# A hybrid recurrent layer on one core: blocks of 16 instead of 8 inverted on VectorE, a refitted list scheduler, and GpSimd's large products on ScalarE and VectorE

## The chip, the cores and the metric

One Trainium2 chip, one core of it. The metric is the device time of one launch in microseconds (us): 1104.89 us is the median of three runs of the kernel before (1103.22 to 1105.05). Below, PE is TensorE, PEld its weight loads, DVE VectorE, ACT ScalarE, POOL GpSimd and SP SyncE, whose queue issues nearly all transfers.

## The reference

One decoder layer for 256 prompt tokens and 8 sequences of 8 new tokens, 320 columns in all. One projection of the normalised input (2048 to 12416 columns) feeds two recurrences; both are projected back, gated, summed, and sent through one output projection.

```python
h = rms_norm(x, norm_g)
p = jnp.einsum('nld,dp->nlp', h, w_in)
...
# branch A, 16 heads of 64, per token
sa = jnp.einsum('nhvk,nhk->nhv', s, kk_t)
s = (s * w_t[:, :, None, :] - sa[..., None] * (kk_t * a_t)[:, :, None, :]
     + v_t[..., None] * k_t[:, :, None, :])
y_t = jnp.einsum('nhvk,nhk->nhv', s, r_t)
...
merged = (sigmoid(p[..., OFF_GA:OFF_GB]) * jnp.einsum('nlw,wd->nld', y_a, proj_a)
          + sigmoid(p[..., OFF_GB:]) * jnp.einsum('nlw,wd->nld', y_b, proj_b))
y = x + jnp.einsum('nld,de->nle', merged, w_out)
```

Branch A is computed in chunks of 64 tokens. Inside a chunk the delta rule is a unit lower triangular system of 64 by 64, so the kernel needs the inverse of such a matrix for each head and chunk. The sequences of 8 new tokens give diagonal blocks of 8 by 8.

## The kernel before, in words

**The stream.** Weights come in tiles of 1024 by 128 by DMA (`raw`, three buffers). ACT rounds each to a high part `whi`, DVE subtracts to get the low part `wlo`, and each of the 16 blocks of 128 rows takes three products of 128 by 320 into PSUM (`mps`, two buffers): high by high, high by low, low by high. These are the products `mps<-...`. A half tile has 24, a column tile 48.

**The recorded part.** After a first tile, 71 column tiles are not issued directly. `tile_of` (L1465 stands for every recorded instruction, because they are issued from one line at the end) records their loads, casts and products, and between them the work of eight steps p = 0 to 7, each with two heads of branch A (`rwkv`) and one of branch B (`hgrn`). `Recorder.add` gives each recorded operation a duration in ns (`o.cost`) and a time until its result can be used (`o.lat`). `link` finds what depends on what. `order` is a list scheduler: it plays the five engines against each other with these durations and so writes down one order per engine. On the chip each engine then runs its list in order and waits at semaphores. A product of the stream goes where nothing small is ready, so how many `mps` products stand between two small ones is the planner's estimate of how long the other engines need. `MARGIN` is an extra time that the planner adds before a small product on PE may stand.

**The inverse.** In `rwkv`, `g2` holds the 64 by 64 matrices. ACT copies their triangles to `nd`; POOL masks out the diagonal blocks of 8 by 8 (`lows`), DVE folds them into `dn` (768 rows of 8), and two transfers through DRAM (`scratch[0]`) lay each block out on one partition (`nb`, 96 blocks). DVE inverts the blocks there with elementwise products and sums (`y8`, doubling 2 to 4 to 8). Two more transfers through `scratch[1]` bring the inverses back (`ye`), POOL spreads them into `yd` and `ys`, ACT copies `yd` into `yz`. From there PE doubles the block size: `for sz in (8, 16, 32)` makes two transposes of `yd`, two products `M` by `yz` (`a<-yz,uE` in the trace) and two products `a<-pp,uB`, with a mask on DVE and a subtraction on DVE between.

**Around it.** After the inverse the first transposes, chunk recurrences (`chunks`: `rhs`, `uv`, `st`) and the sample part (`samples`) follow, then the norm of branch A (`jr_cent`, `jr_mean`) and `ya`. Four recorded tiles after the last step fill sigmoid gates, three more go to DRAM (`late`). The second stage (`L362` to `L364`) is not recorded: it streams the remaining gate columns and, from `split(ya)` on, the products `ppa` and `ppb` with `proj_a` and `proj_b`. The third stage (`po`) multiplies by `w_out`.

**GpSimd's products.** POOL also computes `bm` (128x512) in `samples`, `vm` (96x512, twice) in `hgrn`, `lows` and `yd` (128x256), each a broadcast product of two SBUF operands.

Of the kernel before, what the change touches and what calls it, by code (L numbers as in the profile page):

```python
# [69 lines left out]
class Recorder:  # L70
    APART, MARGIN, WAIT, OVER = 10, 250, 6000, 130
    LAT = {"PE": 215, "V": 45, "S": 45, "G": 80, "Y": 0}
# [13 lines left out]
    def add(self, eng, name, fn, args, kw):  # L86
        o = Op()
        o.eng, o.fn, o.args, o.kw, o.n = eng, fn, args, kw, len(self.ops)
        aps = [x for x in (*args, *kw.values()) if hasattr(x, "start_partition")]
        out = aps[0]  # L90
        free = 1
# [51 lines left out]
        elif eng == "S":  # L143
# [3 lines left out]
            if any(tuple(x.shape[1:]) == (1,) and free > 1 for x in aps[1:]):  # L147
                o.cost += 60
        elif eng == "G":
            o.cost = 950 if "dma" in name else 95 + free * 0.88 if name == "memset" else 200 + free * 1.66  # L150
            if "dma" in name:
                o.lat = 4500
        else:
            o.cost, o.lat = 380, 2600 if any(u[0].startswith("scr") for u in o.uses) else 5500
        self.ops.append(o)
        return o

    def link(self):

        writers, readers, preds = {}, {}, {}  # L160
        for o in self.ops:
            o.succ, pred = [], {}
            preds[o.n] = pred
            for name, p0, p1, m, wr, psum in o.uses:
# [47 lines left out]
    def order(self):  # L212
# [17 lines left out]
        def choose(e):  # L230
# [29 lines left out]
            can = [o for o in q if (at_[o] if e in port else o.ready) <= t_ + 30]  # L260
# [6 lines left out]
            return t_, max(can, key=worth)  # L267
# [30 lines left out]
def hybrid_step(ctx, tc, x_prompt, x_sample, state_rwkv, state_hgrn, state_shift, norm_g, w_in,  # L298
# [80 lines left out]
    with tc.tile_pool(name="start", bufs=1) as st, \  # L379
# [63 lines left out]
        id8 = ctile([128, 64], "id8")  # L443
        G.memset(id8, 0.0)
        G.memset(id8[:, 0:64:9], 1.0)
# [5 lines left out]
        lvs = st.tile([128, 3, 32], F32, name="lvs")  # L451
        lvz = ctile([128, 3, 2, 32], "lvz")
# [4 lines left out]
        for n, sz in enumerate((8, 16, 32)):  # L457
# [11 lines left out]
        G.tensor_copy(seqm[HS[1]], seqm[low_])  # L469

# [314 lines left out]
    def rwkv(p, r, k, vp, za):  # L785
# [132 lines left out]
        for h in range(2):  # L918
            for c_ in range(2):
# [3 lines left out]
        lows = at("lows", (128, 4, 8, 8), tag="pp")  # L923
        each = lambda n: seqm[:, None, :, None].to_broadcast([128, n, 8, 8])
        G.tensor_mul(lows, nd.rearrange("p a h (b j) -> p (a h) b j", j=8), each(4))
        dn = at("dn", (128, 6, 8))
        V.tensor_reduce(dn[:, 0:4], lows.rearrange("p c b j -> p c j b"), axis=mybir.AxisListType.X, op=ALU.add)
        V.tensor_reduce(dn[0:64, 4:6], g2[0:64, 4, 0].rearrange("p h (b j) -> p h j b", j=8),
                        axis=mybir.AxisListType.X, op=ALU.add)
        there = lambda t_: t_.rearrange("(c p) j -> p c j", c=6)  # L930
        whole = lambda t_: t_.rearrange("(q i) j -> q (i j)", i=8)
        Y.dma_start(there(scratch[0]), dn)
        nb = at("nb", (96, 64), tag="pp")
        Y.dma_start(nb, whole(scratch[0]))
        y8 = at("y8", (96, 64))
        V.tensor_sub(y8, id8[:96], nb)

        t8 = nb
        four = lambda o_, *d: bass.AP(y8.tensor, y8.offset + o_, [y8.ap[0], *d])
        t4 = t8[:, 0:4].rearrange("p (a i) -> p a i", i=2)  # L940
        V.tensor_mul(t4, four(2, [36, 2], [8, 2]), four(19, [36, 2], [0, 2]))
        V.tensor_add(four(3, [36, 2], [8, 2]), four(3, [36, 2], [8, 2]), t4)
        V.tensor_mul(t4, four(10, [36, 2], [1, 2]), four(1, [36, 2], [0, 2]))
        V.tensor_add(four(2, [36, 2], [1, 2]), four(2, [36, 2], [1, 2]), t4)
        t64 = t8.rearrange("p (i j k) -> p i j k", j=4, k=4)
        p16 = at("p16", (96, 4, 4))
        V.tensor_mul(t64, four(4, [8, 4], [0, 4], [1, 4]), four(36, [0, 4], [1, 4], [8, 4]))
        V.tensor_reduce(p16, t64, axis=mybir.AxisListType.X, op=ALU.add)
        V.tensor_mul(t64, four(0, [8, 4], [0, 4], [1, 4]),
                     p16.rearrange("p k j -> p j k")[:, None].to_broadcast([96, 4, 4, 4]))  # L950
        V.tensor_reduce(four(4, [8, 4], [1, 4]), t64, axis=mybir.AxisListType.X, op=ALU.add)
        Y.dma_start(whole(scratch[1]), y8)
        ye = at("ye", (128, 6, 8))
# [730 lines left out]
```

## Time and profile before

| what | value |
|---|---|
| median of three runs | 1104.89 us |
| profiled execution | 1104.54 us, of which the span is 1102.8 us |
| PE busy | 1081.3 us, 98% |
| DVE busy | 750.6 us, 68% |
| ACT busy | 680.1 us, 62% |
| POOL busy | 154.6 us, 14% |
| DMA | 161.62 MB, mean 147 GB/s |

The busy time of PE is made of overlapping products: one `mps` product lasts 0.31 us in the trace, and the next starts 0.147 us after it. So the cost of an extra product is read from the starts, not from its length. A wait shows as idle time ahead of an instruction, with what released it. The span divides into a start (to 27 us), the recorded part (to about 690 us, the first stage's tail reaching into the second), the second stage, and the third (from about 975 us).

### The profile page before, as it was taken

Reading aid. Unit: us, or ns where it says so; the run is one execution under the profiler, and the core shown is the slowest. Engines: PE = TensorE matmul, PEld = TensorE weight load, DVE = VectorE, ACT = ScalarE, POOL = GpSimd, SP = SyncE. Lnnn points to the kernel's source line nnn. Section 1 sums busy time; section 2 is a strip of 40 time slices with the busy share of each in tenths; the row PEclk is TensorE's granted clock in tenths of the full one; section 3 lists DMA queues with packets and bytes.
Section 4 is the critical chain, followed back from the end, with each engine's and each line's share of the span. In section 5 each row is a group of like instructions: output and inputs, shape, how many; then the busy total and the mean of one; then the engine's idle time right before and its main releaser. Section 6 shows DMA issues by size and latency. Waiting matters only on the chain.

```text
span 1102.8 us, 23134 instructions
## 1 busy us (share of the span) xinstructions
PE 1081.3 (98%) x9020; PEld 1043.5 (95%) x9020; DVE 750.6 (68%) x1639; ACT 680.1 (62%) x1530; POOL 154.6 (14%) x328
## 2 busy tenths in 40 slices
PE   7999999999999999999999999999999999999996
PEld 6999999999998999999999999999999999998886
DVE  8878787888787788788887976644444444437532
ACT  8767776766865867857857867544444444435412
POOL 6421222311211211211311210000000000000000
PEclk9999999999999999999999999999999999999999
DMA  6743644654553554555445454555555555586502
GB/s 200 205 127 100 180 129 123 161 145 114 162 136 101 156 144 117 153 138 140 117 138 144 123 144 130 149 152 160 152 146 146 149 154 153 153 282 223 200 21 96
DMA packets 298386, 161.62 MB, mean 147 GB/s; under 512 B 37341, under 2 KB 288480, under 8 KB 297700
## 3 DMA queue, kind: packets, MB, share of 16 engines
q1 hardware_dynamic: 297908, 158.83, 50.1%
q8 instruction: 71, 1.16, 0.4%
q10 hardware_dynamic: 368, 1.31, 0.3%
q14 instruction: 39, 0.32, 0.1%
HBM read 149.41 MB, written 10.70 MB: 145 GB/s over the span
## 4 chain that ended last, share of the span: by engine, by line
PE 95%; ACT 2%; DMA 1%; DVE 1%; issue 0%; POOL 0%; DVEq 0%; SPq 0%; ACTq 0%
PE mps L1465 45%; PE a L1465 9%; PE mps L362 5%; PE mps L364 5%; PE mps L363 5%; PE b L1465 3%; PE po L1555 3%; PE po L1556 3%; PE po L1557 3%; PE ppa L363 2%; PE ppa L364 2%; PE ppa L362 2%; PE ppb L362 2%; PE ppb L363 2%; PE ppb L364 2%; PE y L1465 1%
## 5 line engine op out<-in xcount | busy, mean ns | idle before, releaser
L1465 PE MATMUL mps<-hhi,wlo 128*128 128x320 f32 x1136 | 358.9, 316 | 0.0
L1465 PE MATMUL mps<-hhi,whi 128*128 128x320 f32 x1136 | 357.0, 314 | 0.5 <-ACT pad L1465 0.5
L1465 PE MATMUL mps<-hlo,whi 128*128 128x320 f32 x1136 | 357.3, 314 | 0.0
L1465 PEld LDWEIGHTS mps<-hhi,wlo 128*128 128x128 f32 x1136 | 213.7, 188 | 2.3 <-issue 1.5
L1465 PEld LDWEIGHTS mps<-hhi,whi 128*128 128x128 f32 x1136 | 213.8, 188 | 2.0 <-issue 0.8
L1465 PEld LDWEIGHTS mps<-hlo,whi 128*128 128x128 f32 x1136 | 213.7, 188 | 1.5 <-issue 0.8
L1465 DVE TENSOR_TENSOR wlo<-raw,whi 128x1024 fp32r<-128x1024 f32 x140 | 173.6, 1240 | 21.0 <-ACT whi L1465 19.7
L1465 ACT CAST whi<-raw 128x1024 fp32r<-128x1024 f32 x140 | 146.4, 1045 | 63.2 <-PE mps L1465 56.7
L352 ACT CAST whi<-raw 128x1024 fp32r<-128x1024 f32 x82 | 86.0, 1049 | 147.8 <-PE mps L363 94.3
L353 DVE TENSOR_TENSOR wlo<-raw,whi 128x1024 fp32r<-128x1024 f32 x82 | 100.5, 1225 | 110.1 <-ACT whi L352 110.1
L362 PE MATMUL mps<-hhi,whi 128*128 128x320 f32 x400 | 123.9, 310 | 1.0 <-ACT whi L352 1.0
L364 PE MATMUL mps<-hhi,wlo 128*128 128x320 f32 x400 | 123.7, 309 | 0.2 <-DVE wlo L353 0.2
L363 PE MATMUL mps<-hlo,whi 128*128 128x320 f32 x400 | 123.8, 309 | 0.0
L362 PEld LDWEIGHTS mps<-hhi,whi 128*128 128x128 f32 x400 | 75.1, 188 | 1.3 <-ACT whi L352 1.3
L364 PEld LDWEIGHTS mps<-hhi,wlo 128*128 128x128 f32 x400 | 75.1, 188 | 0.4 <-DVE wlo L353 0.4
L363 PEld LDWEIGHTS mps<-hlo,whi 128*128 128x128 f32 x400 | 75.2, 188 | 0.0
L1544 DVE TENSOR_TENSOR wlo<-raw,whi 128x1024 fp32r<-128x1024 f32 x32 | 38.4, 1222 | 36.0 <-ACT whi L1543 35.8
L1543 ACT CAST whi<-raw 128x1024 fp32r<-128x1024 f32 x32 | 33.1, 1052 | 47.7 <-PE po L1560 21.1
L1555 PE MATMUL po<-whi,mhi 128*128 128x512 f32 x128 | 50.0, 391 | 0.0
L1556 PE MATMUL po<-whi,mlo 128*128 128x512 f32 x128 | 50.0, 391 | 0.0
L1557 PE MATMUL po<-wlo,mhi 128*128 128x512 f32 x128 | 50.0, 391 | 0.0
L362 PE MATMUL ppa<-yah,whi 128*128 128x320 f32 x128 | 40.1, 314 | 0.1
(444 smaller groups left out, 2100.2 us busy)
## 6 DMA issues: line engine op xcount, KB each, us to landing
raw<-in_w_in_dram SPq DMA_DIRECT2D x194, 512.0 KB
raw<-in_w_out_dram SPq DMA_DIRECT2D x32, 512.0 KB
raw<-in_proj_a_dram SPq DMA_DIRECT2D x16, 512.0 KB
raw<-in_proj_b_dram SPq DMA_DIRECT2D x16, 512.0 KB
s<-in_state_hgrn_dram SPq DMA_DIRECT2D x8, 512.0 KB
out_dram<-s SPq DMA_DIRECT2D x8, 512.0 KB
s<-in_state_rwkv_dram SPq DMA_DIRECT2D x8, 256.0 KB
out_dram<-s SPq DMA_DIRECT2D x8, 256.0 KB
```

Of the source, the lines that this page charges most:

```text
L352: S.copy(hi[:, ks], raw[:, ks])
L353: sub.tensor_sub(lo[:, ks], raw[:, ks], hi[:, ks].bitcast(F32))
L362: T.matmul(dst, hi[:, q, :], xhi[:, k, :], start=(k == 0), stop=False)
L363: T.matmul(dst, hi[:, q, :], xlo[:, k, :], start=False, stop=False)
L364: T.matmul(dst, lo[:, q, :], xhi[:, k, :], start=False, stop=(k == nk - 1))
L1465: o.fn(*o.args, **o.kw)
L1543: S.copy(hi, raw)
L1544: V.tensor_sub(lo, raw, hi.bitcast(F32))
L1555: T.matmul(pt, h, hi, start=first, stop=False)
L1556: T.matmul(pt, l, hi, start=False, stop=False)
L1557: T.matmul(pt, h, lo, start=False, stop=end)
```

## The change

**Blocks of 16.** `dn` gets 16 columns, 48 partitions hold a block of 16 by 16 each, and DVE inverts them in the layout `y16`: a scaling to the negative, ones on the diagonal by a POOL memset, the step to 2 by 2 as before, and for n = 4 and n = 8 a product, a sum, a product, a sum on n by n by n elements (twice for n = 4). The loop on PE is `for sz in (16, 32)`.

**Engines.** `lows`, `yd` and `ys` go from POOL to DVE. `bm` and `vm` become four ACT operations each with a per-partition scale. Seven copies and scalings of 64x64 per step (two of `rhs`, five of `uv`) go from DVE to ACT, and five small copies (`fh`, `fq`) from DVE to POOL.

**The planner.** Its durations are refitted: for an output on all 128 partitions a part of the duration (`DRAIN`) moves from the engine's time to the time until the result can be used; sums over the free axis cost by the number of inputs; two accesses of different engines to one PSUM bank are ordered. `MARGIN` goes from 250 to 400. `order` may leave an engine idle up to `AHEAD` = 300 ns for an operation of higher rank, filling the gap with one that is short enough.

```diff
-    APART, MARGIN, WAIT, OVER = 10, 250, 6000, 130
-    LAT = {"PE": 215, "V": 45, "S": 45, "G": 80, "Y": 0}
+    APART, MARGIN, WAIT, OVER = 10, 400, 6000, 45
+    AHEAD, SLIP = 300, 0
+    LAT = {"PE": 215, "V": 40, "S": 40, "G": 65, "Y": 0}
+    DRAIN = {"V": 85, "S": 100, "G": 65}
...
+        if eng in self.DRAIN and not o.dma:
+            if name == "tensor_reduce":
+                n = 1
+                for d in aps[1].shape[1:]:
+                    n *= d
+                o.cost += (n - free) / 0.96
+            if out.shape[0] == 128:
+                o.cost -= self.DRAIN[eng]
+                o.lat += self.DRAIN[eng]
+            else:
+                o.cost += 13
...
-                        if hit(u):
+                        if hit(u) or psum and u[3].eng != o.eng:
...
-                q.succ.append((o, data))
+                q.succ.append((o, data or q.eng in self.DRAIN and q.eng != o.eng))
...
-            can = [o for o in q if (at_[o] if e in port else o.ready) <= t_ + 30]
+            best = max((o for o in q if at_[o] <= t_ + self.AHEAD), key=worth)
+            if at_[best] > t_ + 30:
+                short = [o for o in q if at_[o] <= t_ + 30 and at_[o] + o.cost <= at_[best] + self.SLIP]
+                if short:
+                    best = max(short, key=worth)
+            return t_, best
...
-        lows = at("lows", (128, 4, 8, 8), tag="pp")
+        lows = at("lows", (128, 4, 4, 16), tag="pp")
-        G.tensor_mul(lows, nd.rearrange("p a h (b j) -> p (a h) b j", j=8), each(4))
+        V.tensor_mul(lows, nd.rearrange("p a h (b j) -> p (a h) b j", j=16), each(4))
...
-        V.tensor_sub(y8, id8[:96], nb)
+        V.tensor_scalar(y16, nb, -1.0, 0.0, op0=ALU.mult, op1=ALU.add)
+        G.memset(y16[:, 0:256:17], 1.0)
...
+        for n in (4, 8):
+            t_ = at("t3", (48, n, n, n), tag="big")
+            pw_ = at("p64", (48, n, n), tag="uQ")
+            for o_ in range(0, 16, 2 * n):
+                at_ = lambda i, j: 17 * o_ + 16 * i + j
+                V.tensor_mul(t_, four(at_(0, n), [16, n], [0, n], [1, n]), four(at_(n, n), [0, n], [1, n], [16, n]))
+                V.tensor_reduce(pw_, t_, axis=mybir.AxisListType.X, op=ALU.add)
+                V.tensor_mul(t_, four(at_(0, 0), [16, n], [0, n], [1, n]),
+                             pw_.rearrange("p k j -> p j k")[:, None].to_broadcast([48, n, n, n]))
+                V.tensor_reduce(four(at_(0, n), [16, n], [1, n]), t_, axis=mybir.AxisListType.X, op=ALU.add)
...
-        for sz in (8, 16, 32):
+        for sz in (16, 32):
...
-            G.tensor_mul(bm, bk[:, 4, None].to_broadcast([128, 4, 128]), seq4[:, :, None].to_broadcast([128, 4, 128]))
+            for si in range(4):
+                S.activation(bm[:, si], bk[:, 4], AF.Copy, scale=seq4[:, si:si + 1])
...
-            G.tensor_mul(vm[0:96], v3[:, g, None].bitcast(F32).to_broadcast([96, 4, 128]),
-                         seq4[0:96, :, None].to_broadcast([96, 4, 128]))
+            for si in range(4):
+                S.activation(vm[0:96, si], v3[:, g].bitcast(F32), AF.Copy, scale=seq4[0:96, si:si + 1])
```

The order of before on DVE, in the third step (p = 2), where the blocks of 8 are inverted: `y` is `y8`, `pp` and `p` are its scratch, `R`, `F`, `w` and `o` belong to the other branch.

```order
L1465 TENSOR_TENSOR pp_515<-y_0_517 96x4
L1465 TENSOR_TENSOR F_529<-F_529 128x8x16
L1465 TENSOR_TENSOR y_0_517<-y_0_517,pp_515 96x2x2
L1465 TENSOR_TENSOR w_0_531<-w_0_531,q_483 128x16x8
L1465 TENSOR_TENSOR pp_515<-y_0_517 96x64
L1465 TENSOR_TENSOR w_0_531<-w_0_531,f_485 128x16x8
L1465 TENSOR_TENSOR wlo<-raw,whi 128x1024
L1465 TENSOR_REDUCE p_0_518<-pp_515 96x16
L1465 TENSOR_TENSOR R_530<-R_530,F_529 128x4x32
L1465 TENSOR_TENSOR pp_515<-y_0_517,p_0_518 96x64
L1465 TENSOR_TENSOR F_529<-F_529 128x4x32
L1465 TENSOR_REDUCE y_0_517<-pp_515 96x4x4
```

The same place on DVE in the changed kernel: `uK` is now `y16`, `big` holds the n by n by n products, `uQ` their sums.

```order
L1489 TENSOR_TENSOR big_511<-uK_490 48x64
L1489 TENSOR_REDUCE uQ_472<-big_511 48x16
L1489 TENSOR_TENSOR wlo<-raw,whi 128x1024
L1489 TENSOR_TENSOR big_511<-uK_490,uQ_472 48x64
L1489 TENSOR_REDUCE uK_490<-big_511 48x4x4
...
L1489 TENSOR_TENSOR big_511<-uK_490 48x512
L1489 TENSOR_REDUCE uQ_472<-big_511 48x64
L1489 TENSOR_TENSOR wlo<-raw,whi 128x1024
L1489 TENSOR_TENSOR big_511<-uK_490,uQ_472 48x512
L1489 TENSOR_REDUCE uK_490<-big_511 48x8x8
```

Before, an operation of the other branch or of the weights stands behind nearly every operation of the inversion. Now its 17 operations stand together, with two `wlo` between them and nothing else, and the two pairs on 512 elements are new.

The order of before on PE at the end of the recorded part: the last small product of the last step (`jr_mean`) stands among products of the second stage, and the first product that needs all of `ya` (`ppa`) comes 23 rows later.

```order
L362 MATMUL mps<-hhi,whi 128x320
L1465 MATMUL a_497<-rl_495,jr_mean 128x320
L363 MATMUL mps<-hlo,whi 128x320
...
L363 MATMUL mps<-hlo,whi 128x320
L362 MATMUL ppa<-yah,whi 128x320
L364 MATMUL mps<-hhi,wlo 128x320
```

The same place in the changed kernel:

```order
L1489 MATMUL mps<-hhi,wlo 128x320
L1489 MATMUL a_494<-rl_492,jr_mean 128x320
L1489 MATMUL mps<-hhi,whi 128x320
...
L383 MATMUL mps<-hlo,whi 128x320
L382 MATMUL ppa<-yah,whi 128x320
L383 MATMUL ppa<-yal,whi 128x320
```

The last small product now stands among recorded products (L1489, the new number of L1465), and 145 rows lie between it and the first `ppa` instead of 23. In the middle of the program the distance on PE from a step's `a<-arp,bk` products to its first transposes of `yd` is nearly what it was: on average 161 `mps` products before and 167 now (third step: 165 and 174).

More of the change, by code (lines that the diff above doesn't have):

```diff
@@ L259, in choose @@
                 return max(t_, o.ready), o
-            can = [o for o in q if (at_[o] if e in port else o.ready) <= t_ + 30]
+            if e not in port:
+                at_ = {o: max(now, o.ready) for o in q}
             def worth(o):
@@ L940, in rwkv @@
[L940 to L947, printed above, removed]
@@ L1362, in hybrid_step @@
     scr = ctx.enter_context(tc.tile_pool(name="scr", bufs=1, space=bass.MemoryType.DRAM))
-    scratch = [scr.tile([768, 8], F32, name=f"scr{j}", tag=f"scr{j}") for j in range(2)]
+    scratch = [scr.tile([768, 16], F32, name=f"scr{j}", tag=f"scr{j}") for j in range(2)]
     late = [scr.tile([128, NT], F32, name=f"scrg{m}", tag=f"scrg{m}") for m in range(NLATE)]
```

64 lines of the change are left out of this document (32 added, 32 removed).

## The prediction, made before the changed kernel had run

> **What bounds the kernel now.** I read the page first: the span, the busy times and the chain that ended last.
>
> ```profile
> span 1102.8 us, 23134 instructions
> PE 1081.3 (98%) x9020; PEld 1043.5 (95%) x9020; DVE 750.6 (68%) x1639; ACT 680.1 (62%) x1530; POOL 154.6 (14%) x328
> PE 95%; ACT 2%; DMA 1%; DVE 1%; issue 0%; POOL 0%; DVEq 0%; SPq 0%; ACTq 0%
> ```
>
> PE is the bound: the chain that set the end is PE work for 95%. So only two kinds of time can change: products that PE no longer makes, and waits in which PE stands still. Next I read the windows by stage. The columns are the stretch, its length, and the busy time of PE, PEld, DVE, ACT and POOL with their instructions, then the granted clock, the DMA share and GB/s.
>
> ```profile
> 27.00:660.00 633.00, 628.00 (x6120) 614.81 (x6119) 513.59 (x1291) 460.29 (x1160) 135.70 (x280) 1.00 0.50 139
> 660.00:694.00 34.00, 32.31 (x311) 30.02 (x309) 23.24 (x57) 25.72 (x69) 1.66 (x2) 1.00 0.49 139
> 694.00:699.00 5.00, 4.78 (x21) 4.55 (x22) 4.21 (x7) 4.55 (x9) 0.00 (x0) 0.66 0.55 164
> 699.00:1060.00 361.00, 361.00 (x2264) 346.78 (x2263) 173.11 (x206) 158.29 (x227) 0.00 (x0) 1.00 0.54 165
> ```
>
> From 699 us on PE has no gap and the change touches nothing there. In the recorded part PE lacks 5.0 us of 633, and at its seam with the second stage 1.7 us of 34 and a stretch of 5 us at a clock of 0.66. Third, the waits of PE between 27 and 700 us: what waited, for whom, us in total, times, longest.
>
> ```profile
> PE b L1465 <- issue: 1.9, 1, 1.9
> PE a L1465 <- DVE yz L1465: 1.2, 2, 0.6
> PE a L1465 <- POOL yd L1465: 1.0, 1, 1.0
> PE mps L362 <- ACT whi L352: 1.0, 1, 1.0
> PE a L1465 <- ACT uv L1465: 0.5, 1, 0.5
> PE mps L1465 <- ACT pad L1465: 0.5, 1, 0.5
> PE a L1465 <- issue: 0.4, 1, 0.4
> PE mps L364 <- DVE wlo L353: 0.2, 1, 0.2
> ```
>
> Six gaps (issue, yz twice, yd, pad, issue) lie before 660 us: 1.9 + 1.2 + 1.0 + 0.5 + 0.4 = 5.0 us. Three (whi, uv, wlo) lie in the seam: 1.7 us. A gap costs more than its idle time, because the overlap of the products is lost too:
>
> ```profile
> 691.92 0.31 PE L364 MATMUL mps<-hhi,wlo 128*128 128x320 f32 x1
> 693.22 0.41 PE L362 MATMUL mps<-hhi,whi 128*128 128x320 f32 x1 [0.99 <-ACT whi L352]
> ```
>
> Start to start this is 1.30 us where undisturbed products are 0.147 apart (below), so 1.15 lost with 0.99 idle: 0.16 us more per gap.
>
> **Part 1: one doubling less on PE.** The step for size 8 goes: per step p two transposes of `yd`, two products `a<-yz,uE` and two `a<-pp,uB` (each product of 128x128 in full float32 is two records). The timeline of PE shows what they cost inside the stream: start, duration, line, tile.
>
> ```profile
> 167.48 0.31 PE L1465 MATMUL mps<-hhi,whi 128*128 128x320 f32 x1
> 167.63 0.38 PE L1465 MATMUL a<-ident,yd 128*128 128x128 f32 x2
> ...
> 167.99 0.31 PE L1465 MATMUL mps<-hhi,wlo 128*128 128x320 f32 x1
> ...
> 168.29 0.31 PE L1465 MATMUL mps<-hlo,whi 128*128 128x320 f32 x1
> 168.44 0.61 PE L1465 MATMUL a<-yz,uE 128*128 128x128 f32 x4
> 168.80 0.39 PE L1465 MATMUL mps<-hhi,wlo 128*128 128x320 f32 x1
> 169.03 0.31 PE L1465 MATMUL mps<-hhi,whi 128*128 128x320 f32 x1
> ...
> 169.76 0.31 PE L1465 MATMUL mps<-hhi,wlo 128*128 128x320 f32 x1
> 169.90 0.61 PE L1465 MATMUL a<-pp,uB 128*128 128x128 f32 x4
> ...
> 170.50 0.30 PE L1465 MATMUL mps<-hlo,whi 128*128 128x320 f32 x1
> ```
>
> From 169.03 to 169.76 lie five products of the stream, 0.146 each. The transposes stretch two such steps (0.29) to 167.99 - 167.48 = 0.51: 0.22 us. The two pairs stretch two steps to 169.03 - 168.29 = 0.74 and 170.50 - 169.76 = 0.74: 0.45 us each, the slow first product after them (0.23 instead of 0.147) included. So a level costs 0.22 + 0.45 + 0.45 = 1.12 us, and over eight steps **-8.9 us**. Nothing hides this: PE has no other gap to put it in. At most it is 0.6 us less, where such products stand beside other small ones and share the switch of 0.08 us.
>
> **Part 2: the seam.** In the order of before 23 PE rows lie between the last small product of step 7 and the first `ppa`, now 145. So the tail of step 7 is done some 122 x 0.147 = 18 us earlier against the stream, and the splitting of `ya`, behind which ACT and DVE make the second stage's weights, lies beside stream products. The three gaps cost 1.7 + 3 x 0.16 = 2.2 us. In 694 to 699 us there are 21 products where 34 would fit; 13 x 0.147 = 1.9, less 0.4 for the gap at `wlo` already counted: 1.5 us. I let both go: **-3.7 us**. Late next is nothing that the profile shows before 1060 us. The clock is the weaker half: it read 1.00 in the other three stretches, so also around the gap of 1.9 us, and fell here, where three gaps lie close together. [...]
>
> **Part 3: the longer chain on DVE.** Instead of PE, DVE doubles from 8 to 16. That costs no PE time unless the first transposes of a step wait. In the third step, the one with the gap at `yd`, the chain of before was this (one row from each place):
>
> ```profile
> 233.14 0.22 DVE L1465 TENSOR_TENSOR y<-id,pp 96x64 f32<-96x64 f32 x1
> 239.12 0.21 DVE L1465 TENSOR_REDUCE y<-pp 96x16 f32<-96x64 f32 x1
> 239.35 0.33 SPq L1465 DMA_DIRECT2D scr<-y  x1
> 242.36 0.37 SPq L1465 DMA_DIRECT2D ye<-scr  x1
> 247.22 1.25 POOL L1465 TENSOR_TENSOR yd<-ye,seqm 128x256 f32<-128x256 f32 x1 [2.35 <-DMA ye<-scr]
> ```
>
> DVE took 239.33 - 233.14 = 6.2 us, nine short operations with others between; the transfers 3.0 and 4.9 us; POOL 1.25. Prices for the new DVE work come from groups of before (count, then busy us and mean ns):
>
> ```profile
> L1465 DVE TENSOR_TENSOR y<-id,pp 96x64 f32<-96x64 f32 x8 | 1.7, 218 | 0.2
> L1465 DVE TENSOR_TENSOR pp<-y 96x64 f32<-96x64 f32 x8 | 2.2, 274 | 0.0
> L1465 DVE TENSOR_REDUCE p<-pp 96x16 f32<-96x64 f32 x8 | 1.7, 209 | 0.0
> L1465 DVE TENSOR_REDUCE dn<-pp 128x32 f32<-128x256 f32 x8 | 5.3, 659 | 4.0 <-POOL pp L1465 4.0
> L1465 DVE TENSOR_TENSOR wlo<-raw,whi 128x1024 fp32r<-128x1024 f32 x140 | 173.6, 1240 | 21.0 <-ACT whi L1465 19.7
> L1465 ACT CAST whi<-raw 128x1024 fp32r<-128x1024 f32 x140 | 146.4, 1045 | 63.2 <-PE mps L1465 56.7
> ```
>
> Read in order, an element costs (1240 - 218) / 960 = 1.06 ns, so 512 elements take 0.70 us. That is the low bound. The products of the inversion read one operand in steps of a row: 274 instead of 218 for 64 elements, 0.88 ns per element more, so 512 take 0.70 + 0.45 = 1.15 us. The sum `dn<-pp`, also read in steps, has 659 for 256 elements where 218 + 192 x 1.06 = 422 would do: 0.93 ns more, the same price. I take 1.15 for the two products and 0.70 for the two sums, which read in order. [...]
>
> The chain is then: the scaling of 256 elements 0.42, four operations on 8 elements 0.6 (an estimate under the 0.21 of 64 elements), four pairs on 64 elements 4 x (0.27 + 0.21) = 1.9, the two pairs on 512 2 x 1.15 + 2 x 0.70 = 3.7, and the two `wlo` that the order puts between, 2 x 1.15 = 2.3: 8.9 us instead of 6.2. Against that, `lows` and `yd` as DVE operations of 128x256, some 0.42 us each by the same price, in place of POOL's (1.25 here): about 1.0 us saved in all. The transfers carry twice the bytes in the same number of pieces or fewer, 64 bytes instead of 32 at the small end; nothing in the trace prices this, between 0 and 1 us more. I take 0. So the chain grows by 1.7 us, and the order gives it 167 instead of 161 products on average, 6 x 0.147 = 0.9 us more. That leaves 0.8 us less room per step. One step in eight waited before; in the others there was room, how much I leave open. If all eight lacked the 0.8, that would be 6.4 us; if only the third did, 0.8. I take **+1.5 us** for it. The other five gaps before 660 us I leave as they are: they lie in chains that the change only reorders, with 150 ns more margin but durations that are closer and so leave less unplanned room.
>
> **Part 4: other moved work.** `bm` and `vm` go to ACT: twelve operations on 128 columns per step, each between nothing and half a cast (0.5 us), so at most 6 us of a step's 633 / 8 = 79. ACT was busy 460 of 633 us, with 22 us free per step, and its wait of 56.7 us in the row above is for PE to release `whi`, so casts are ahead of the stream and this costs 0. If that cover went, each late cast would cost what the gap at `whi` cost, 1.15 us. What queues behind: `bm` shares its buffer with the n by n by n products, so ACT now waits there for the end of DVE's chain, with a cast behind it. POOL, busy 136 of 633 us, gives four large products away for five small copies and a memset of the diagonal, which costs nothing on PE. SP has as many transfers as before.
>
> **The sum.** -8.9 - 3.7 + 1.5 = -11.1 us on the profiled execution of 1104.54 (its span of 1102.8 and 1.7 around it), which lies 0.35 us under the median of the runs, so I make no correction: **1093.4 us**.
>
> **The rivals.** *All gaps close.* The planner's new durations fit, and its margin of 400 catches the rest. For it, the timeline of DVE:
>
> ```profile
> 229.96 1.22 DVE L1465 TENSOR_TENSOR wlo<-raw,whi 128x1024 fp32r<-128x1024 f32 x1
> 231.10 1.33 DVE L1465 TENSOR_TENSOR R<-F 128x320 f32<-128x320 f32 x1
> ```
>
> `wlo` holds DVE for 1.14 us and ends at 1.22; the old plan held DVE for 1024 / 0.96 + 157 = 1224 ns, the new one for 85 less. Against it: the gap at `issue` of 1.9 us has no releaser that a plan could move, and strided reads are not in the new durations either. 1104.5 - 8.9 - 3.7 - (5.0 + 6 x 0.16 = 6.0) = 1085.9 us. Chance 0.2.
>
> *Products go, gaps move.* ACT, loaded with up to 6 us more per step and waiting at `bm`, makes casts or `pad` copies late about once a step, at the price of the gap at `pad`, 0.5 + 0.16 = 0.66: 8 x 0.66 = 5.3 us on top, 1098.7 us. Chance 0.18. For it: ACT stood behind three of the nine gaps. Against it: its 56.7 us of room.
>
> *Slower: every step's first transposes wait.* PE takes its list in order, so when `yd` is late the whole stream stands. With a wait w in each step the time is 1104.5 - 12.6 - 1.2 + 8w. It is no gain from w = 1.7 us, and slower by more than 0.2% from w = 2.0. Reaching that takes the 0.8 of part 3 without the room of the seven other steps, transfers 1 us slower, and 0.5 from waiting for POOL's memset in the chain; at their sum, w = 2.3, it is 1109.1 us. Against it: that room was there in seven of eight steps, and the order sets the margin anew. Chance 0.12, half of it within 0.2%.
>
> **How the numbers follow.** The forecast, 1090 to 1097, has 0.5. The range takes in the first rival at 1085.9 with 1.4 us of doubt in parts 1 and 3 and the second at 1098.7 with the clock's 1.5 us: 1084.5 to 1100.5, leaving out most of the third. 0.2%, 2.2 us, is about what a measurement of this kernel can tell from no change. Faster by more than that: 0.5 + 0.2 + 0.18 = 0.88; within it 0.06; slower 0.06.
>
> **What would show it.** In the new profile: 32 records fewer each of `a<-yz,uE` and `a<-pp,uB`; no PE gap between the last recorded product and `ppa`, and a clock of 1.00 there; DVE products on 512 elements at 1.1 to 1.2 us; waits of PE on DVE `yd` of 1 to 5 us in all. It is wrong if waits on `yd` or `whi` exceed 9 us, or if the recorded part is not shorter by about the level's 8.9 us plus the difference in gaps.

## The result, and the profile after

The changed kernel takes 1097.48 us (median of 5 runs, 1095.81 to 1100.13), the kernel before in the same comparison 1105.05 us (5 runs, 1103.22 to 1106.62): a ratio of 0.9929, 95% interval 0.9908 to 0.995. The forecast was 1093.4 us, 4.1 less. The profiled execution took 1097.48 us too, so it stands for the median.

The page of the changed kernel, then its windows by stage (columns as before):

```profile
span 1095.8 us, 23048 instructions
PE 1072.2 (98%) x8940; PEld 1035.4 (94%) x8940; DVE 764.8 (70%) x1607; ACT 723.5 (66%) x1658; POOL 113.3 (10%) x325
PE 83%; DVE 8%; ACT 4%; issue 2%; DMA 2%; DVEq 0%; SPq 0%; ACTq 0%
```

```profile
27.00:660.00 633.00, 624.47 (x6079) 610.27 (x6078) 538.55 (x1300) 513.87 (x1329) 96.23 (x282) 1.00 0.51 140
660.00:687.00 27.00, 27.00 (x271) 26.74 (x270) 11.74 (x14) 13.94 (x25) 0.00 (x0) 1.00 0.55 160
687.00:694.00 7.00, 5.78 (x38) 5.52 (x38) 6.08 (x8) 6.97 (x12) 0.00 (x0) 1.00 0.44 133
694.00:1060.00 366.00, 366.00 (x2281) 350.51 (x2280) 175.69 (x211) 158.93 (x230) 0.00 (x0) 1.00 0.54 164
```

PE has 80 records fewer, and is still the bound. But between 27 and 660 us it now lacks 8.5 us where it lacked 5.0, and 1.2 us are still missing at the seam. Which waits those are, from the view of PE's waits between 27 and 700 us:

```profile
PE b L1489 <- issue: 4.6, 3, 2.1
PE a L1489 <- DVE yd L1489: 2.8, 5, 0.7
PE mps L1489 <- issue: 1.0, 1, 1.0
PE ppa L382 <- ACT yah L1511: 0.8, 1, 0.8
PE ppa L383 <- DVE yal L1512: 0.4, 1, 0.4
```

The waits on `yz`, `uv`, `pad`, `whi` and `wlo` are gone. The waits on `yd` went from one to five. And "issue", time in which PE waits for nothing that the profile shows, went from 2.3 us to 5.6. The timeline of PE has these four places (idle time in brackets):

```profile
173.38 0.26 PE L1489 MATMUL b<-ks,s 128*32 128x64 f32 x3 [1.30 <-issue]
252.81 0.22 PE L1489 MATMUL b<-ket 128*32 128x32 f32 x2 [1.14 <-issue]
330.80 0.24 PE L1489 MATMUL b<-ks,s 128*32 128x64 f32 x1 [2.12 <-issue]
409.98 0.30 PE L1489 MATMUL mps<-hhi,wlo 128*128 128x320 f32 x1 [1.01 <-issue]
```

All four stand at or behind the end of the same piece of work, the burst of some 140 small records that one call of `side_by_side` issues in each step; the four other steps have no such wait. Behind the longest of them, the window of 3.5 us shows a granted clock of 0.51:

```profile
332.00:335.50 3.50, 3.50 (x16) 3.50 (x15) 2.29 (x9) 2.69 (x11) 0.21 (x1) 0.51 0.02 5
```

The 16 products in it would be 24 at 0.147 us; the drop costs some 1.7 us (3.4 us at half speed). Before, such a drop stood at the seam; there the clock is now 1.00.

The seam, from ACT's timeline: the last gate tile `f` is made, and the first cast of the split waits.

```profile
681.30 0.97 ACT L1489 ACTIVATE f<-f 128x320 f32<-128x320 f32 x2
687.03 2.61 ACT L1511 CAST yah<-ya 128x640 fp32r<-128x640 f32 x4 [2.58 <-DMA scrg<-f]
```

What `yah` waits for is not step 7's chain, but the transfer that writes `f` to DRAM: `yah` takes SBUF that `f` gives up.

### The profile page after: what moved, and what is told of

Read it like the earlier page. It is cut to its first block, busy times and chain, and to the rows that moved or that the text cites. A ratio compares the mean times of both kernels' runs of the same rounds, so it can differ in the third digit from the quotient of the medians.

```text
span 1095.8 us, 23048 instructions
## 1 busy us (share of the span) xinstructions
PE 1072.2 (98%) x8940; PEld 1035.4 (94%) x8940; DVE 764.8 (70%) x1607; ACT 723.5 (66%) x1658; POOL 113.3 (10%) x325
## 3 DMA queue, kind: packets, MB, share of 16 engines
q8 instruction: 70, 1.15, 0.4%
## 4 chain that ended last, share of the span: by engine, by line
PE 83%; DVE 8%; ACT 4%; issue 2%; DMA 2%; DVEq 0%; SPq 0%; ACTq 0%
PE mps L1489 34%; PE a L1489 8%; PE mps L382 5%; PE mps L384 5%; PE mps L383 5%; PE b L1489 3%; PE po L1579 3%; PE po L1580 3%; PE po L1581 3%; DVE wlo L1489 3%; PE ppa L383 2%; PE ppb L382 2%; PE ppb L383 2%; PE ppb L384 2%; PE ppa L384 2%
## 5 line engine op out<-in xcount | busy, mean ns | idle before, releaser
L1489 PE MATMUL mps<-hhi,wlo 128*128 128x320 f32 x1136 | 358.2, 315 | 1.0 <-issue 1.0
L1489 PE MATMUL mps<-hhi,whi 128*128 128x320 f32 x1136 | 357.8, 315 | 0.0
L1489 PE MATMUL mps<-hlo,whi 128*128 128x320 f32 x1136 | 357.1, 314 | 0.0
L1489 PEld LDWEIGHTS mps<-hhi,whi 128*128 128x128 f32 x1136 | 214.1, 188 | 2.3 <-issue 1.5
L1489 PEld LDWEIGHTS mps<-hlo,whi 128*128 128x128 f32 x1136 | 214.2, 189 | 2.1 <-issue 1.5
L1489 PEld LDWEIGHTS mps<-hhi,wlo 128*128 128x128 f32 x1136 | 214.2, 189 | 1.9 <-issue 1.2
L1489 DVE TENSOR_TENSOR wlo<-raw,whi 128x1024 fp32r<-128x1024 f32 x140 | 170.7, 1220 | 24.4 <-ACT whi L1489 22.7
L1489 ACT CAST whi<-raw 128x1024 fp32r<-128x1024 f32 x140 | 145.7, 1042 | 26.6 <-PE mps L1489 24.0
```

The lines of the kernel that those rows point to most:

```text
L1489: o.fn(*o.args, **o.kw)
```

## The experiments

Two theories for the missing 4.1 us. *Instruction stream:* the waits at "issue" depend on where in PE's instruction stream a burst begins. The page's row of the queue that carries instructions (packets, MB, share) says in what pieces they come:

```profile
q8 instruction: 70, 1.15, 0.4%
```

1.15 MB in 70 packets is 16.4 KB each; PE has 8,940 weight loads, as many products and some 80 waits in its stream, 17,960 in all. If these bytes are PE's alone, one takes 64 and a piece holds 256: an estimate from the row and the counts. Against it: *place in the program*: the bursts coincide with transfers, ACT's load or an order that the planner made worse. They are told apart by products of 32x32 that are put on PE at the start: they move every later instruction in the stream and, beyond a later start, change nothing else. "Position" means the count of PE's instructions at the burst's first product, modulo 256.

**84 tiny products ahead of the changed kernel.**

```diff
             V.memset(ones.bitcast(F32), 1.0)
+            for _ in range(84):
+                T.matmul(wps[:32, :32], ones[:32, :32], ones[:32, :32], start=True, stop=True)
```

> The changed kernel with 84 tiny products (32x32, one record each) put on PE at the start, where PE has nothing to do. In the changed kernel PE stands 5.6 us in all at 173, 253, 331 and 410 us, each time at the end of the burst of some 140 small records of a step and each time with no releaser. Theory (instruction stream): PE's instructions come in pieces of 256, and a burst that crosses from one piece to the next at the wrong place uses a piece up before the next is there. Counted from the first instruction of PE, modulo 256, the eight bursts start at 142, 190, 199, 180, 151, 109, 115, 74 now; the four that stand are those between 145 and 205. 84 records more are 168 instructions more: 54, 102, 111, 92, 63, 21, 27, 242. By this theory all four waits go, 5.6 + 4 x 0.16 = 6.2 us, and with them the drop of the granted clock behind the longest, about 1.8 us: 1089.5 us (1088.5 to 1091.5). Rival (place in the program: transfers, load of ACT, the planner's order): the order is the same, so the four waits stay and the time is that of the changed kernel, 1097.5, or up to 5 us more if the 84 products delay the start.

1094.73 us (ratio to before 0.9897, 0.9881 to 0.9913). Its waits of PE between 27 and 720 us, whole:

```profile
PE a L1491 <- DVE yd L1491: 4.5, 7, 1.4
PE ppa L382 <- ACT yah L1513: 0.6, 1, 0.6
PE ppa L383 <- DVE yal L1514: 0.4, 1, 0.4
```

No wait at "issue" is left, and the clock stays at 1.00: the theory holds, the rival doesn't. The time missed the 1089.5 because the tiny products did delay the start, and the waits on `yd` grew by 1.7 us. The start is read from one early product that all kernels have, first in the changed kernel, then in this one:

```profile
24.59 0.27 PE L683 MATMUL cps<-ident,rows 128*128 128x128 f32 x1
```

```profile
28.04 0.27 PE L685 MATMUL cps<-ident,rows 128*128 128x128 f32 x1
```

From there to the first `ppa` the changed kernel takes 663.2 us, this one 657.0. The sum closes: 1097.5 - 6.2 (waits with lost overlap) - 1.7 (clock) + 3.4 (start) + 1.7 + 2 x 0.16 (`yd`) = 1095.0, 0.3 off the measured time.

**22 of them.** The same edit with 22, which fit into the time in which PE waits for its first operands and cost 0.15 us of start.

> The changed kernel with 22 tiny products on PE at the start: the bursts start at 186, 234, 243, 224, 195, 153, 159, 118 modulo 256. Theory (instruction stream): the waits move, to the steps 0, 4, 5 and 6 (186, 195, 153, 159), and steps 1, 2, 3 and 7 have none; about the changed kernel's time, 1095 to 1099 us. Rival (place in the program): the waits stay in the steps 1, 2, 3 and 4 at about 173, 253, 331 and 410 us.

One run, 1092.7 us, below the 1095 to 1099 expected. Waits at "issue": 1.45 us at 92.9 (step 0) and 1.42 us at 557.4 (step 6); none in the other steps. So the waits did move, but to two of the four steps named. The position alone is too coarse a rule. The trace has a finer one. Each window of the DMA view in which the instruction queue moved a packet brackets its start to 0.1 us; for the wait at 173.38 in the changed kernel these are the rows of 170.8 to 170.9 and of 174.5 to 174.6 us:

```profile
q8 instruction: 1, 0.02, 61.6%
q8 instruction: 1, 0.02, 73.3%
```

One piece starts at 170.9, PE runs dry at 172.1 and goes on at 173.4, and the next piece starts at 174.6. Read so for all kernels here, the 14 waits at "issue" that stand at a burst end 2.3 to 2.7 us after such a packet starts, and no two packets start closer than 3.2 us. A burst of 280 instructions runs in some 2 us where nothing holds it (2.06 us from 481.25 us in the changed kernel). In 13 of the 14 the next piece starts 3.4 to 4.2 us after that packet, in one (669 us in the next kernel) 8.2 us. Pairs at 3.6 us without a wait exist too, so a close pair alone does not make a wait, and what makes a piece come late is not shown. Three waits at "issue" of 0.4 to 0.6 us, ahead of products `a<-pp,uB`, stand 12 us or more behind a packet and are of another kind; the 0.4 us of the kernel before is one of them.

**98 of them ahead of the kernel before.**

> The kernel before with 98 tiny products on PE at the start and nothing else. Its bursts start at 250, 78, 96, 186, 250, 210, 224, 255 now, with one wait of 1.9 us in step 3 (186); with 196 instructions more at 190, 18, 36, 126, 190, 150, 164, 195. Theory (instruction stream): waits of 1 to 2 us in the steps 0, 4, 5, 6 and 7 and none in step 3, so 4 waits more of about 1.5 + 0.16 us each: some 6.6 us slower than the kernel before, 1111 us (1108 to 1114). Rival (place in the program): the wait of 1.9 us stays in step 3 and the time is 1105.

1114.94 us, 1.008 of the kernel before (1.0063 to 1.0096), just above the 1108 to 1114 expected. The wait in step 3 is gone; the steps 0, 4, 5, 6 and 7 have waits of 0.58, 1.94, 0.23, 0.71 and 1.78 us. Of the 10.4 us between the profiled executions 4.2 are the later start (28.85 against 24.63), 3.3 the waits at "issue" (2.3 before, 5.6 now) and 1.1 the waits on `yd`, before the lost overlap. An edit that adds no work behind the start thus made the same program slower, in part through these waits. Beside it, the lesson for part 2: the clock dropped for 3.4 us after the 1.78 and not after the 1.94, so the length of a gap alone does not decide it. The drops in the kernel before (0.50 from 695.16 to 698.57 us), in the changed one and in this one are 3.41 us long each; what sets that length is not shown.

**The seam: the gates that go to DRAM first.**

```diff
-        for m in range(NFILL):
-            tile_of(OFF_GA + 128 * m, lambda ps, m=m: sigm(sga[:, m, :], ps))
         for m, (pool, key) in enumerate(((at, "za"), (bt, "q"), (bt, "f"))[:NLATE]):
...
             tile_of(OFF_GA + 128 * (NFILL + m), post)
+        for m in range(NFILL):
+            tile_of(OFF_GA + 128 * m, lambda ps, m=m: sigm(sga[:, m, :], ps))
```

> The changed kernel with the last seven tiles of the recorded part in another order: the three whose gates go to DRAM first, the four that stay in SBUF last; and 45 tiny products at the start, which by the first theory keep all bursts (142, 187, 172, 165, 191, 136, 142, 187 without them) clear: 232, 21, 6, 255, 25, 226, 232, 21. Theory for the seam: its two waits (0.8 and 0.4 us) come from the transfer of the last gate tile to DRAM, whose SBUF the first cast of the split takes; with that transfer early they go, 1.7 us with the lost overlap: 1089.5 - 1.7 = 1087.8 us, and no wait at the first ppa. Rival for the seam: step 7's chain or ACT's load sets it, and the waits stay at about 1.2 us: 1089.5.

1090.45 us (0.9859, 0.984 to 0.9878). All waits of PE between 27 and 720 us:

```profile
PE a L1491 <- DVE yd L1491: 3.9, 6, 1.3
```

The seam is clean and no wait at "issue" is left, so the transfer of `f` was the cause at the seam. Against the expected 1087.8 stand a start that is 1.4 us later and the waits on `yd`.

**The waits on `yd`: a price for strided reads.**

```diff
+            far = [x for x in aps[1:] if "PSUM" not in str(x.space) and [s for s, c in x.ap[1:] if c > 1][-1:] > [3]]
+            if far:
...
+                o.cost += n * 0.88
```

> The changed kernel; its planner now adds 0.88 ns per element to a DVE operation that reads SBUF in inner steps of more than three elements (the price that the trace shows). 8 of the 20 products that warm PE up at the start are replaced by 33 tiny ones, which takes about as long and puts the bursts at 230, 6, 6, 21, 222, 250, 227, 253 modulo 256, clear of the instruction waits. Beside it stands the changed kernel with 84 tiny products, which has no instruction waits either: 1094.7, of which some 3.4 us are its later start, so 1091.3. Theory: the waits on yd, 4.5 us there, come from a chain on DVE that takes longer than its planner thinks; with the price they fall below 1 us: 1087.5 us (1086 to 1089). Rival: they come from the transfers before yd or from PE's own arrival, which the price does not touch: they stay at 2.5 to 4.5 us, 1091.

1087.38 us (0.9842, 0.9827 to 0.9857), as expected, and no wait on `yd`:

```profile
PE ppa L388 <- ACT yah L1519: 1.1, 1, 1.1
PE ppa L389 <- DVE yal L1520: 0.4, 1, 0.4
```

Behind these two gaps the clock drops again: it reads 0.50 from 678.3 to 681.6 us.

**A control: the same time, spread over all DVE operations.**

```diff
+            o.cost += 10
```

> A control for the price: the changed kernel, whose planner adds 10 ns to every DVE operation (some 190 of them per step, 1.9 us, about what the price for reads in steps adds to one step's chain of DVE, but not there), and 34 tiny products at the start, which put the bursts at 244, 255, 8, 254, 216, 239, 235, 239 modulo 256. Theory (the waits on yd come from the price that is missing in the chain before yd): the waits on yd stay at 2 to 5 us, 1091 us (1090 to 1093). Rival (any new order, or any slack on DVE, removes them): below 1 us, 1088.

1089.29 us (0.9847, 0.9828 to 0.9866); waits on `yd` 1.8 us in four steps. Neither side is met: less than the 2 to 5 expected, more than the rival's 1.

**All three together.** Price, order of the gates, and 22 tiny products.

> The three causes taken together: the price of 0.88 ns per element for DVE's reads in steps, the three gates that go to DRAM ahead of the four that stay in SBUF, and 22 tiny products at the start, which put the bursts at 224, 0, 0, 15, 216, 2, 13, 34 modulo 256, clear of the instruction waits. The kernel with the price alone took 1087.4 us; it had waits of 1.1 and 0.4 us at the seam, 1.8 with the lost overlap, and a stretch of 3.4 us at half the clock just behind them, 1.7 us. Theory: both go, and 0.4 us of its later start: 1083.5 us (1082.5 to 1085). Rival for the clock: it drops on its own account somewhere: 1085.2. Rival for the seam: the other order brings waits of its own, 1087.

1088.06 us (0.9832, 0.9815 to 0.985): no gain over the price alone. The seam is clean, the clock stays at 1.00, there is no wait at "issue". But `yd` is back, in two steps:

```profile
PE a L1497 <- DVE yd L1497: 3.5, 2, 2.1
```

The planner is the one with the price, and PE's order is the same into step 4 (to 400 us) but for one swap; the other order of the gates reached back into the last steps. DVE's timeline shows that here it is the transfer that is late:

```profile
552.02 0.43 DVE L1497 TENSOR_TENSOR yd<-ye,own 128x256 f32<-128x256 f32 x1 [2.29 <-DMA ye<-scr]
631.05 0.42 DVE L1497 TENSOR_TENSOR yd<-ye,own 128x256 f32<-128x256 f32 x1 [2.17 <-DMA ye<-scr]
```

So the price is not shown to be what removed the waits; with it they stayed out in one order and not in the other.

**The planner waits longer for the small transfers.**

```diff
-            o.cost, o.lat = 380, 2600 if any(u[0].startswith("scr") for u in o.uses) else 5500
+            o.cost, o.lat = 380, 4600 if any(u[0].startswith("scr") for u in o.uses) else 5500
```

> The kernel with the three causes taken together, which took 1088.1 us, with one number of the planner changed: the small transfers through DRAM land after 380 + 4600 ns, not 380 + 2600. 22 tiny products ahead and 38 in place of 7 that warm PE up put the bursts at 130, 244, 119, 83, 44, 5, 220, 87 modulo 256, clear of the instruction waits. In the kernel with the three causes PE waited 3.5 us for yd in steps 6 and 7, and there DVE waited 2.3 and 2.2 us for the transfer of ye, which came 3.9 and 4.6 us after its issue where the planner has 3.0. Theory (the rest of the waits on yd is the landing of the two transfers): the waits on yd go, 3.5 + 0.3 us: 1084.2 us (1083 to 1085.5). Rival (yd's waits are a matter of where the plan happens to put the chain, whatever it takes the transfers for): waits on yd of 2 us or more somewhere, 1087 or more.

1138.82 us, 1.0303 of the kernel before (1.0288 to 1.0317). The waits on `yd` are gone, and something worse has come. PE's waits, the first two rows:

```profile
PE mps L1499 <- ACT pad L1499: 24.3, 4, 6.5
PE mps L1499 <- ACT i L1499: 6.7, 4, 1.9
```

One of the four, followed from PE to ACT to DVE:

```profile
339.54 0.64 PE L1499 MATMUL mps<-hhi,whi 128*128 128x320 f32 x1 [5.98 <-ACT pad L1499]
```

```profile
333.45 1.04 ACT L1499 CAST whi<-raw 128x1024 fp32r<-128x1024 f32 x1 [2.47 <-PE mps L1499]
337.53 1.28 ACT L1499 ACTIVATE big<-bk,seq 128x128 f32<-128x128 f32 x4 [3.03 <-DVE uK L1499]
339.00 0.49 ACT L1499 COPY pad<-mps 128x256 f32<-128x256 f32 x2 [0.19 <-DVE r L1499]
```

```profile
335.71 1.07 DVE L1499 TENSOR_TENSOR big<-uK,uQ 48x512 f32<-48x512 f32 x1
336.81 0.68 DVE L1499 TENSOR_REDUCE uK<-big 48x64 f32<-48x512 f32 x1
337.52 0.33 DVE L1499 TENSOR_TENSOR fq<-f,fh 32x8 fp32r<-32x8 f32 x2
337.87 0.50 DVE L1499 TENSOR_TENSOR dif<-pad 128x328 f32<-128x328 f32 x1
338.41 0.69 DVE L1499 SCALAR_TENSOR_TENSOR r<-dif,cols,pad 128x256 f32<-128x256 f32 x2
```

PE's bank of PSUM is full until ACT copies it into `pad`. ACT takes its list in order, and ahead of that copy stands `bm` (`big<-bk,seq`), whose buffer DVE's chain still reads: `bm` starts when the last sum ends. But `bm` is done at 338.81, and the copy still waits, for DVE's `r`. There is one `pad`; `dif` and `r` read what it held before, and they stand behind the whole chain in DVE's list. So without `bm` the copy would have started no earlier: what holds PE for 6 us is the chain on DVE ahead of the readers of `pad`. It is so in all four waits. Behind the wait the clock is at half besides (0.50 from 339.54 to 343.20 us, some 1.8 us lost). Neither theory had that.

**The planner alone, on the kernel before** (the class `Recorder` of the changed kernel in the program before, and 93 tiny products in place of 20 that warm PE up).

> The kernel before with the planner of the changed kernel alone (blocks of 8 and POOL's products stay), and the 20 products that warm PE up replaced by 93 tiny ones, which puts the bursts at 30, 56, 38, 43, 2, 7, 222, 212 modulo 256, clear of the instruction waits. Theory (the planner closes its gaps, the level's work is a separate 8.9 us): the waits at yz, yd, pad, uv and whi (4.1 us idle, 5.1 us with the lost overlap) go, the instruction waits of 2.3 us too, the clock's drop at the seam (1.5 us) too; some 1.2 us at the seam and 1 us on yd come in: 1105 - 5.1 - 2.6 - 1.5 + 2.2 = 1098 us (1096 to 1100). Rival (the new durations move gaps only): only the instruction waits go: 1102.5.

1099.41 us (0.9948, 0.993 to 0.9965): the theory, within its range. PE's waits in it are 2.4 us in five places, and it starts 2.1 us later than the kernel before (26.68 against 24.63).

**The large products `bm` and `vm` back on POOL** (as before; the same 93 tiny products).

> The changed kernel with the products bm and vm back on POOL, as before, and 93 tiny products for the 20 that warm PE up, which puts the bursts at 42, 38, 52, 8, 16, 245, 17, 214 modulo 256, clear of the instruction waits. Theory (the twelve ACT operations per step lie beside PE's work): on PE nothing changes by it, 1091.3 us as the changed kernel without instruction waits (1090 to 1093). Rival (POOL's large products hold DVE's port and delay its chain): waits on yd grow to 8 us or more, 1095 or more. Second rival (ACT's load costs the changed kernel time): faster than 1089.5.

1097.25 us (4 runs, 1094.71 to 1099.16; 0.9929, 0.9907 to 0.9951), its profiled execution 1094.71. Its waits on `yd` are 3.9 us in three steps, 5.7 us in seven places in all. So neither rival's sign: POOL's products do not push `yd` to 8 us, and the kernel is not faster than 1089.5. `port` is the planner's name for DVE's operations and POOL's holding each other up. The kernel before has such a place: `R<-F` on 128x320 takes 1.33 us at 231.10, beside `bm` on POOL (230.31 to 232.09 us), where the median of its eight is 0.48. But the time misses the theory's 1090 to 1093 too. Of the 1094.7 of the profiled execution 2.1 are a later start; what makes the other runs up to 4.5 us longer is not shown, and it hides any small effect of ACT's load. Beside the kernel before with the new planner this one has the blocks of 16 and the other moves between DVE, ACT and POOL, with the same tiny products, the same start (26.70 against 26.68 us), the same 3468 `mps` products ahead of the first `ppa` and the same engine for `bm` and `vm`: to the first `ppa` it takes 658.1 us against 663.0, 5.0 less, with 5.7 + 7 x 0.16 = 6.8 us of waits against 2.4 + 5 x 0.16 = 3.2. Without the waits the blocks and the moves are worth 5.0 + 3.6 = 8.6 us; of the two, the level alone takes work from PE.

**The change with the planner of before.**

> The changed kernel with the planner of the kernel before; 20 tiny products at the start put the bursts at 238, 85, 223, 252, 0, 5, 174, 34 modulo 256, so that only step 6 can have an instruction wait (some 1.5 us). Theory (a level of 8 steps is worth 8.9 us whatever the planner): 1105 - 8.9, less the instruction waits of before 2.3 plus 1.5 here, and the gaps of the old planner stay or grow by up to 3 us on yd: 1096 to 1099 us. Rival (without its own durations the longer chain on DVE makes every step's transposes of yd wait, 1 us or more each): 1104 or more.

1127.68 us, 1.0208 of the kernel before (1.0183 to 1.0233): the theory falls, and the rival's time comes by another way than the rival's. Not `yd` but this stands first:

```profile
PE mps L1471 <- ACT pad L1471: 17.4, 3, 7.5
PE mps L1471 <- ACT za L1471: 4.4, 4, 1.4
```

Two of the three waits on `pad`, on ACT:

```profile
503.05 1.28 ACT L1471 ACTIVATE big<-bk,seq 128x128 f32<-128x128 f32 x4 [2.90 <-DVE uK L1471]
505.95 0.49 ACT L1471 COPY pad<-mps 128x256 f32<-128x256 f32 x2 [1.63 <-DVE k L1471]
```

```profile
585.98 1.28 ACT L1471 ACTIVATE big<-bk,seq 128x128 f32<-128x128 f32 x4 [2.72 <-DVE uK L1471]
590.61 0.49 ACT L1471 COPY pad<-mps 128x256 f32<-128x256 f32 x2 [3.35 <-DVE k L1471]
```

`bm` has waited 2.9 and 2.7 us for DVE's last sum, and the copy then waits 1.6 and 3.4 us more, for DVE's `k`, which reads `pad` as `r` does above. In the third, `bm` waited 0.3 and the copy 2.4. So here, too, DVE's list is what ends last. The clock is at half for up to 10 us at such a stop (0.50 from 584.7 to 594.8 us).

**And with one term of the new planner** (a sum costs by what it reads).

> The changed kernel with the planner of before, which took 1127.7 us, and one term of the new planner: a DVE sum costs by the elements that it reads, not by those that it writes. 72 tiny products for 15 of those that warm PE up put the bursts at 84, 217, 252, 246, 19, 29, 255, 126 modulo 256. Theory (the old planner takes the sums of 512 elements for 0.22 us where they take 0.67, so DVE runs behind the plan, and ACT with it at bm): most of the 22 us go, 1100 us (1096 to 1105). Rival (the other refitted terms are what counts: drains, the bank of PSUM, the short work ahead of a late one): it stays above 1115.

1123.72 us (1.0156, 1.0135 to 1.0177), `pad` still 16.6 us, in five waits: 4 of the 22 us by the times, some 6 by the ratios. That theory falls too; which of the other terms (drains, the bank of PSUM, short work ahead of a late one) keeps the readers of `pad` in time is open.

## Why the prediction was right, and where it was off

The sign, the main term and the range were right. By its steps:

*Part 1, the level:* held. The groups of PE's small products have the records forecast (96 and 48 before), and the content of the change, of which the level is the part on PE, is worth 8.6 us where the prediction had 8.9:

```profile
L1489 PE MATMUL a<-yz,uE 128*128 128x128 f32 x64 | 10.0, 279 | 0.0
L1489 PE MATMUL a<-pp,uB 128*128 128x128 f32 x64 | 9.8, 276 | 0.0
L1489 PE MATMUL a<-ident,yd 128*128 128x128 f32 x32 | 6.5, 285 | 3.0 <-DVE yd L1489 2.8
```

*Part 2, the seam:* this step failed. The three gaps were to go because step 7's chain is done some 18 us earlier. It is: the last `jr_mean` product stands 22 us ahead of the first `ppa` (665.6 and 687.8 us) where it stood 5 us ahead. And yet 1.2 us of gaps stayed. The prediction asked what is late next and answered "nothing that the profile shows"; it was the buffer that `yah` takes over from the last late tile, behind a transfer to DRAM. With the gates in another order the gaps are gone. The clock's drop left the seam, as forecast, but came back behind the gap of 2.12 us at 331: a gain of 1.5 forecast, none had. That it would go with the gaps was the author's estimate; the runs show it behind some gaps and not behind others as long, and not what decides it.

*"The other five gaps before 660 us I leave as they are":* wrong in both directions. Those at `yz` (two) and `pad`, 1.7 us idle and 2.2 with the lost overlap, went, as the first rival had it. The two at "issue", the longer of which was said to have no releaser that a plan could move, became four, from 2.6 to 6.2 us with the lost overlap. But for the 0.4 us of before, they go with the position of each burst in the instruction stream, and a change that removes 80 records shifts it. This is the largest error, 3.6 us.

*Part 3, the longer chain:* its prices held. The scaling starts at 227.47 us in the third step and the last sum ends at 236.52, 9.05 us where 8.9 was forecast. The groups, forecast at 1.15 us for the products and 0.70 for the sums:

```profile
L1489 DVE TENSOR_TENSOR big<-uK,uQ 48x512 f32<-48x512 f32 x8 | 9.3, 1161 | 0.2
L1489 DVE TENSOR_TENSOR big<-uK 48x512 f32<-48x512 f32 x8 | 8.5, 1058 | 0.2
L1489 DVE TENSOR_REDUCE uK<-big 48x64 f32<-48x512 f32 x8 | 5.4, 675 | 0.2
```

The waits on `yd`, 2.8 us in five steps, lie within the 1 to 5 us named. With the overlap they cost 3.6, and the one of before cost 1.2: +2.4 instead of +1.5. The cause is not settled. In the third step of the changed kernel DVE itself was late, with a `wlo` ahead of `yd` in its list; in the last two steps DVE waited 0.2 and 0.3 us for the transfer, and in the kernel with all three edits the transfer was what came late.

*Part 4, other moved work at no cost:* right for this order. The cover named there is still there, if smaller, and `bm` does wait for the end of DVE's chain:

```profile
L1489 ACT CAST whi<-raw 128x1024 fp32r<-128x1024 f32 x140 | 145.7, 1042 | 26.6 <-PE mps L1489 24.0 <-issue 1.5 <-DVE wlo L1489 0.5
L1489 ACT ACTIVATE big<-bk,seq 128x128 f32<-128x128 f32 x32 | 11.2, 394 | 12.6 <-DVE uK L1489 12.6
```

None of these 12.6 us shows among PE's waits. What the prediction did not have is a second way from the longer chain to PE: the buffer `pad`, whose readers on DVE can stand behind the chain. The second rival priced a late `pad` copy at 0.66 us; where that way was open, the single waits went up to 7.5 us, and the three kernels with it took 18 to 34 us more than the kernel before. Part 3 and the slower rival looked at `yd` alone.

*The sum.* Forecast -8.9 - 3.7 + 1.5 = -11.1; measured 1097.5 - 1104.5 = -7.1. The terms measured: level -8.6, `yz` and `pad` -2.2, `yd` +2.4, "issue" +3.6, seam 2.2 to 1.5 -0.7, clock 0: -5.5. Some 1.6 us of gain are not assigned to any term. That the time fell inside the range is in part luck: the 2.2 and the 1.6 us, which the forecast did not have, stood against the 3.6 at "issue", which it did not have either. Two small slips in the prediction's sums change nothing: eight times 1.12 is 9.0, and the second rival's 1098.7 with the clock's 1.5 is 1100.2. And the parts do not add: the planner alone gave -5.8 us against its own runs of the kernel before, with a start 2.1 us later and the instruction waits moved out, the new content with the old planner +22.5, both together -7.6.

## What to carry to other kernels

Time in which an engine waits for nothing that the profile shows is not a constant of the stage: look at which instruction burst it stands behind and when the instruction queue's packets start, and count it as a term that a change of the instruction count can move: here it was 2.3 us in the kernel before, 5.6 in the changed one and none with 84 tiny products ahead of that. When a stall is said to go, follow not only the chain that ended last but every buffer that the next operation takes over, transfers to DRAM among them. And where a planner's order puts a long chain into the list of an in-order engine, price it by what stands behind it in that list: with the readers of `pad` behind DVE's chain, a PSUM bank was held and PE stood for 6 us. The nearest late operation, here `bm`, need not be the one that ends last.

Of the kernels tried, the one with the price for strided reads is the fastest (1087.4 us); the one with all three edits takes 1088.1, and the intervals of the two overlap.

## What the runs showed of the hardware

- Instructions came in pieces of 16.4 KB (1.15 MB in 70 packets in the changed kernel). PE's burst of some 280 instructions, which took 2.06 us from 481.25 us in the changed kernel, where nothing held it, stood for up to 2.2 us (2.12 at 331 us there, 2.20 in the changed kernel with the planner of before), ending 2.3 to 2.7 us after a piece's transfer started.
- The granted clock fell to half for 3.4 us behind single gaps of 1.78 (98 tiny products ahead of the kernel before) and 2.12 us (the changed kernel) and not behind gaps of 1.94 (98 tiny products ahead of the kernel before), 2.10 (all three edits, at `yd`) and 2.20 us (the planner of before, at "issue").
- In the changed kernel a DVE product of 512 elements on 48 partitions, one operand of which is read in steps of 16 or 8 elements, took 1.06 and 1.16 us, a sum of 512 elements read in order 0.675.
